# Two attentions beside a stream of matmuls: the maximum read as the exponential's bias, roundings on GpSimd, and a changed order of exponentials and fetches

## The chip, the cores and the metric

The kernel runs on one core of a Trainium2 chip. The metric is device time in microseconds of one execution; the figure of a kernel is the median of several runs. The engines are TensorE (PE, its weight loads PEld), VectorE (DVE), ScalarE (ACT), GpSimd (POOL) and SyncE (SP), which here only issues DMAs. Other DMAs are issued from the queues of ScalarE and GpSimd.

## The reference

One layer of a streaming encoder on 512 tokens of 1024 channels, in float32. The change touches the two attentions at its start:

```python
(a_q, a_k, a_v, f_q, f_k, f_v, f_g, ...) = jnp.split(h @ w_in[l], cuts, axis=-1)
# differential attention: 4 heads, two score maps of 64 channels each, chunk-causal mask
s = einsum(q_blk, k) * 64 ** -0.5
p = softmax(where(mask, s, -inf))
a = p[:, :, 0] - lam * p[:, :, 1]
ya = rms_norm(a @ v)
# forgetting attention: 8 heads of 64 channels, causal, with a bias from the cumulated gates
log_f = log_sigmoid(f_g + b_fgt);  c = cumsum(log_f)
s = einsum(q_blk, k) * 64 ** -0.5 + c_q - c_k
p = softmax(where(causal, s, -inf));  yf = p @ v
```

Around them stand a convolution module, a gated short convolution, sigmoid gates and projections of the four branches, an output projection, a cross attention into 256 memory tokens and a gated MLP. All of that runs unchanged before, beside and behind the two attentions.

## The kernel before, in words

**Products.** Matrix products are taken as three fp32r matmuls, each float32 operand being split into a rounded high part and a low rest. `split` (lines 153 to 156) does it for a result in PSUM: ScalarE copies to the high part, VectorE subtracts. `split_weights` does it for weights (line 192 the ScalarE cast of 128x1024, line 193 the VectorE subtraction). High and low are rounded in writing them.

**The main stream.** `run_blocks` (line 209) runs a list of jobs in order. A job has a weights tile to be loaded and a body that issues its matmuls: a group of 24 matmuls of 512 columns for one block of output channels. Three jobs ahead, `fetch` loads the weights by SP and splits them; it stands in front of the body of the current job. Bodies evacuate their PSUM bank at the end. `main` (line 842) records the latest evacuation on ScalarE in `evacuations[0]`.

**The heads beside it.** `Background` holds generators, `a_task` (one for each head h of the first attention, lines 905 on) and `f_task` (one for each pair of heads p of the second, lines 1068 on). Between the matmuls of the main stream, `bg.tick` takes a step of them. Each has 4 steps with scores, one for each tile of 128 queries; query tile qt sees (qt + 1) * 128 keys, so the widths are 128, 256, 384 and 512. A step of `a_task` computes two score maps into PSUM; VectorE adds the mask, writes the sum to `e` and leaves its maximum in the small tile `st` (line 928). A VectorE operation of two columns multiplies the maxima by -1/8 (line 931); ScalarE takes the exponentials with that as bias and leaves their sums (line 933); a reciprocal and scalings follow (lines 935 to 938). `f_task` is the same with a bias tile that GpSimd makes from the cumulated gates (lines 1116 and 1118), the reduction in line 1122, the small operation in line 1125, the exponentials in line 1128.

**Turning the probabilities.** The values need the probabilities with keys on the partitions. The near heads (h = 3, p = 2 and 3) are turned by TensorE (`to_keys_major`). The far ones (h < 3, p < 2) are turned in squares of 32 by VectorE (line 848), stored to DRAM by SP (`put`, line 853) and fetched again in the turned order (`get`, line 860, into `ptl`). `split_in_place` then splits them: ScalarE casts `ptl` to `pth` (line 866, behind the latest evacuation) and VectorE subtracts (line 867). Two steps after its fetch, `values` multiplies them with v, half by half: the first half is for query tiles 0 and 1, the second for 2 and 3. The result is copied (line 947 in `a_task`), turned and normalised. GpSimd does the power operations of the norms (lines 277 and 280) and the clearing of parts of each head's `qk` tile (line 802).

**The values of the second attention** come from `vf_jobs`, four jobs with two channel tiles each (kb = 0 to 3). The last one evacuates eight PSUM banks (`done`, through `split`) and calls `forget_gates`, which computes the cumulated gates, writes them to DRAM (`crows`) and turns them.

**Order.** All this is program order. A scheduler at compile time, with a model of the engines, fixes from it the order of the instructions on each engine, program order being the priority. `tc.issue_after(x)` has what follows take its place behind instruction x in that order; it is no dependency in itself.

Of the kernel before, what the change touches and what calls it, by code (L numbers as in the profile page):

```python
# [17 lines left out]
F32 = mybir.dt.float32  # L18
F32R = mybir.dt.float32r
AF = mybir.ActivationFunctionType  # L20
# [5 lines left out]
P = 128  # L26
# [57 lines left out]
def hybrid_layer(ctx: ExitStack, tc: tile.TileContext, a: dict, out: bass.AP):  # L84
# [121 lines left out]
    def run_blocks(jobs, ahead=3):  # L206

        jobs = iter(jobs)  # L210
        pending = []

        def fetch():
            while True:
                job = next(jobs, None)
                if job is None:
                    return
                if job[1] is None:
                    pending.append((job[0]() if callable(job[0]) else job[0] or (), job[2]))
                else:  # L220
                    pending.append((load_weights(*job[:2], *job[3:]), job[2]))
                if job[0] is not None:
                    return

        for _ in range(ahead):
            fetch()
        while pending:
            if pending[0][0]:
                fetch()
            w, body = pending.pop(0)  # L230
            body(*w)
            bg.tick()

    def matmul(ps, lhs, rhs, start, stop):
# [624 lines left out]
    def get(d, n, pt, local):  # L859
        SP.dma_start(part_of(pt[1], n, local).bitcast(F32), d.rearrange("(a j) (b x) -> (j b) a x", j=32, b=4))  # L860

    def split_in_place(n, pt, local):
        hi, lo = (part_of(x, n, local) for x in pt)
        raw = lo.bitcast(F32)
        with tc.issue_after(evacuations[0]):
            A.copy(hi, raw)
        V.tensor_tensor(lo, raw, hi.bitcast(F32), ALU.subtract)

    def over_channels(ps, x):

# [24 lines left out]
    def a_task(h, qk, v):  # L895
        es, pt, av = {}, None, None
        far = h < 3
        yield 0.0, 3.0
        for step in range(8 if far else 6):
            if step in ((5, 7) if far else (3, 5)):  # L900
                if av is None:
                    av = bank("av")
                vh, vl = (x[:, :, h * P:(h + 1) * P] for x in v[0])
                with tc.issue_after(steps_of[0]) if far else ExitStack():
                    values(av, lambda kt: ((vh[:, kt], 0), (vh[:, kt], 1), (vl[:, kt], 0)), pt,
                           step // 2 - (2 if far else 1))
            cost = 0.0
            if far:
                for qt in SPLITS.get(step, ()):
                    split_in_place(qt + 1, pt, qt % 2)  # L910
                    cost += 0.1 + 0.15 * qt
                for qt in GETS.get(step, ()):
                    if qt % 2 == 0:
                        pt = pt_tiles()
                    get(es.pop(qt)[:, 0], qt + 1, pt, qt % 2)
            elif 1 <= step <= 4:
                if step in (1, 3):
                    pt = pt_tiles()
                to_keys_major(es.pop(step - 1)[:, 0], step, pt, (step - 1) % 2)
                cost += 0.1 + 0.15 * step  # L920
            if step < 4:
                qt, w = step, (step + 1) * P
                e = es[qt] = e4()
                st = m1p.tile([P, 8], F32, tag="st8", name="st8", bufs=4)
                for c in range(2):
                    ps = bank("sc")
                    scores(ps, qk, c, qt * P, w)
                    V.tensor_tensor_reduce(e[:, c, :w], ps[:, :w], mask_a[:, S - w:], scale=1.0,
                                           scalar=-3.0e38, op0=ALU.add, op1=ALU.max,
                                           accum_out=st[:, c:c + 1])  # L930
                V.tensor_scalar(st[:, 2:4], st[:, 0:2], -HD ** -0.5, None, ALU.mult)
                for c in range(2):
                    A.activation(e[:, c, :w], e[:, c, :w], AF.Exp, bias=st[:, 2 + c:3 + c],
                                 scale=HD ** -0.5, accum_out=st[:, 4 + c:5 + c])
                V.reciprocal(st[:, 6:8], st[:, 4:6])
                V.tensor_scalar(st[:, 7:8], st[:, 7:8], lam, None, ALU.mult)
                A.activation(e[:, 1, :w], e[:, 1, :w], AF.Copy, scale=st[:, 7:8])
                V.scalar_tensor_tensor(e[:, 0, :w], e[:, 0, :w], st[:, 6:7], e[:, 1, :w], ALU.mult,
                                       ALU.subtract)
                cost += 0.6 + 0.0035 * w  # L940
                if far:
                    turn_squares(e[:, 1, :w], e[:, 0, :w])
                    es[qt] = put(e[:, 1:], w)
                    cost += 0.0015 * w
            if step == (7 if far else 5):
                e = e4()
                A.copy(e[:, 0], av)
            yield cost, (6.0 if step == 5 else 4.0) if far else 3.5

        ps = bank("tr")  # L950
        for t in range(NT):
            transpose(ps[:, t * P:(t + 1) * P], e[:, 0, t * P:(t + 1) * P])
        A.activation(e[:, 1], ps, AF.Square, scale=1.0 / math.sqrt(P))
        ms = m1p.tile([P, NT], F32, tag="ms4", name="ms4", bufs=2)
        V.tensor_reduce(ms, e[:, 1].rearrange("p (t c) -> p t c", t=NT), AX.X, ALU.add)
        r = rstd_of(m1p, [ms], NT)
        V.tensor_tensor(e[:, 0].rearrange("p (t c) -> p t c", t=NT),
                        ps.rearrange("p (t c) -> p t c", t=NT),
                        r.unsqueeze(2).to_broadcast([P, NT, P]), ALU.mult)
        yield 1.5, 3.5  # L960
        ps2 = bank("tr")
        for t in range(NT):
            transpose(ps2[:, t * P:(t + 1) * P], e[:, 0, t * P:(t + 1) * P])
        if "a" not in y:
            y["a"] = (y8b(), y8b())
        split(ps2, y["a"][0][:, h], y["a"][1][:, h], half["dn"])
        yield 0.6, 0.0
# [5 lines left out]
    def vf_jobs(dst):  # L973
# [20 lines left out]
        for kb in range(4):  # L994
            def body(hi, lo, kb=kb):
                held.append((hi, lo))
                if kb == 0:
                    dst.append(m1p.tile([P, NT, 8, 2, HD], F32R, tag="v", name="v"))
                    dst.append(small["fz_raw"].rearrange("p (t h) -> p t h", t=NT))
                    ps.update({(t, g): bank(("mm", "av")[g]) for t in range(2) for g in range(2)})  # L1000
                products(kb, (0, 1))
                if kb < 3:
                    return
                done(0)
                done(1)
                bg.tick()
                ps.update({(t, g): bank(("mm", "av")[g]) for t in range(2, 4) for g in range(2)})
                for b in range(4):
                    products(b, (2, 3))
                    bg.tick()  # L1010
                done(2)
                done(3)
                forget_gates(dst[1])

            yield *cols(w_in, O_FV, BR + 8, kb * 2, 2), body

    def forget_gates(z_raw):
# [36 lines left out]
    def f_task(p, qk, v):  # L1054
# [19 lines left out]
        for step in range(8 if far else 6):  # L1074
# [33 lines left out]
            if step < 4:  # L1108
# [3 lines left out]
                for j in range(2):  # L1112
                    head = 2 * p + j
                    bias = m1p.tile([P, S], F32, tag="fbias", name="fbias", bufs=2)

                    G.tensor_scalar(bias[:, :w], ck[j][:, :w], -1.0, cq[:, qt, head:head + 1],  # L1116
                                    ALU.mult, ALU.add)
                    G.affine_select(out=bias[:, w - P:w], in_=bias[:, w - P:w], pattern=[[-1, P]],
                                    compare_op=ALU.is_ge, fill=BIG, base=0, channel_multiplier=1)
                    ps = bank("sc")  # L1120
                    scores(ps, qk, j, qt * P, w)
                    V.tensor_tensor_reduce(e[:, j, :w], ps[:, :w], bias[:, :w], scale=1.0,  # L1122
                                           scalar=-3.0e38, op0=ALU.add, op1=ALU.max,
                                           accum_out=st[:, j:j + 1])
                V.tensor_scalar(st[:, 2:4], st[:, 0:2], -HD ** -0.5, None, ALU.mult)
                turn_ready()
                for j in range(2):
                    A.activation(e[:, j, :w], e[:, j, :w], AF.Exp, bias=st[:, 2 + j:3 + j],
                                 scale=HD ** -0.5, accum_out=st[:, 4 + j:5 + j])
                V.reciprocal(st[:, 6:8], st[:, 4:6])  # L1130
                for j in range(2):
                    if j:
# [10 lines left out]

        e = e4()
        for j in range(2):
            A.copy(e[0:HD, j], av[j][HD:P])
            V.tensor_tensor(e[j * HD:(j + 1) * HD, 0], av[j][0:HD], e[0:HD, j], ALU.add)
        split(e[:, 0], y["f"][0][:, p], y["f"][1][:, p])
        yield 1.8, 0.0
# [741 lines left out]
```

## Time and profile before

| | before |
|---|---|
| median of 3 runs | 1050.71 us (1050.49 to 1051.55) |
| profiled execution | 1050.01 us |
| its span in the profile | 1048.2 us |
| granted TensorE clock, mean | 0.999 |
| instructions | 14451 |
| PE busy | 1037.6 us |
| DVE busy | 807.9 us |
| ACT busy | 508.5 us |
| POOL busy | 147.5 us |

The profile is of one execution. The ends of matmuls are modelled in it, so a busy TensorE may hold short waits; starts are recorded. Where the table and the views give a mean duration, it is of all instructions of a group. The first attention runs from about 225 to 350 us, the second from about 380 to 545 us, both beside products of the main stream.

### The profile page before, as it was taken

Reading aid. Unit: us, or ns where it says so; the run is one execution under the profiler, and the core shown is the slowest. Engines: PE = TensorE matmul, PEld = TensorE weight load, DVE = VectorE, ACT = ScalarE, POOL = GpSimd, SP = SyncE. Lnnn points to the kernel's source line nnn. Section 1 sums busy time; section 2 is a strip of 40 time slices with the busy share of each in tenths; the row PEclk is TensorE's granted clock in tenths of the full one; section 3 lists DMA queues with packets and bytes.
Section 4 is the critical chain, followed back from the end, with each engine's and each line's share of the span. In section 5 each row is a group of like instructions: output and inputs, shape, how many; then the busy total and the mean of one; then the engine's idle time right before and its main releaser. Section 6 shows DMA issues by size and latency. Waiting matters only on the chain.

```text
span 1048.2 us, 14451 instructions
## 1 busy us (share of the span) xinstructions
PE 1037.6 (99%) x5255; PEld 882.5 (84%) x5255; DVE 807.9 (77%) x1265; ACT 508.5 (49%) x838; POOL 147.5 (14%) x239
## 2 busy tenths in 40 slices
PE   8999999999999999999999999999999999999997
PEld 8888888888888988888888899998888888888886
DVE  7999998677768369876577898776767777667796
ACT  5322222376465356765443666655343333445662
POOL 4001000100000114432101031121112111111001
PEclk9999999999999999999999999999999999999999
DMA  8953333334433246642357734235577666726662
GB/s 272 315 158 90 102 100 101 99 85 122 137 103 110 61 122 186 181 136 81 101 160 265 237 124 137 63 104 189 191 241 225 217 224 218 220 81 183 215 215 81
DMA packets 182141, 163.86 MB, mean 156 GB/s; under 512 B 17151, under 2 KB 154092, under 8 KB 182069
## 3 DMA queue, kind: packets, MB, share of 16 engines
q1 hardware_dynamic: 173027, 131.18, 42.0%
q10 hardware_dynamic: 6482, 23.21, 6.2%
q0 software_dynamic: 2560, 8.54, 2.5%
q8 instruction: 41, 0.67, 0.3%
q14 instruction: 31, 0.25, 0.1%
HBM read 139.43 MB, written 23.48 MB: 155 GB/s over the span
## 4 chain that ended last, share of the span: by engine, by line
PE 98%; DVE 1%; DMA 0%; ACT 0%; issue 0%; POOL 0%; POOLq 0%; DVEq 0%; SPq 0%; ACTq 0%
PE ps_mm L235 53%; PE ps_av L235 30%; PE ps_sc L235 7%; PE ps_tr L235 4%; PE ps_tr L241 2%; PE ps_mm L453 1%; PE ps_av L453 1%; DMA xs<-in_x 0%; ACT e L735 0%; DVE qk L808 0%; PE ps_tr L437 0%; DVE o L1781 0%; PE ps_av L437 0%; ACT qk L806 0%; DVE e L848 0%
## 5 line engine op out<-in xcount | busy, mean ns | idle before, releaser
L192 ACT CAST wh<-wr 128x1024 fp32r<-128x1024 f32 (+1 forms) x140 | 146.6, 1048 | 261.5 <-PE ps_mm L235 158.2
L193 DVE TENSOR_TENSOR wl<-wr,wh 128x1024 fp32r<-128x1024 f32 (+1 forms) x140 | 174.7, 1249 | 85.5 <-ACT wh L192 85.3
L235 PE MATMUL ps_mm<-hth,wh 128*128 128x512 f32 (+1 forms) x616 | 230.5, 381 | 0.4 <-DVE qk L808 0.2
L235 PE MATMUL ps_mm<-hth,wl 128*128 128x512 f32 (+1 forms) x616 | 229.8, 379 | 0.0
L235 PE MATMUL ps_mm<-htl,wh 128*128 128x512 f32 (+1 forms) x616 | 229.7, 379 | 0.0
L235 PEld LDWEIGHTS ps_mm<-hth,wh 128*128 128x128 f32 x616 | 114.1, 188 | 21.9 <-ACT y L158 0.6
L235 PEld LDWEIGHTS ps_mm<-hth,wl 128*128 128x128 f32 x616 | 114.0, 188 | 21.4
L235 PEld LDWEIGHTS ps_mm<-htl,wh 128*128 128x128 f32 x616 | 114.0, 188 | 20.5
L235 PE MATMUL ps_av<-htl,wh 128*128 128x512 f32 (+1 forms) x328 | 122.5, 373 | 0.0
L235 PE MATMUL ps_av<-hth,wh 128*128 128x512 f32 (+1 forms) x328 | 122.4, 373 | 0.0
L235 PE MATMUL ps_av<-hth,wl 128*128 128x512 f32 (+1 forms) x328 | 122.3, 373 | 0.0
L688 DVE SCALAR_TENSOR_TENSOR y<-y,par,y 128x508 f32<-128x508 f32 (+29 forms) x120 | 82.9, 731 | 0.1
L235 PEld LDWEIGHTS ps_av<-hth,wl 128*128 128x128 f32 x328 | 61.7, 188 | 11.0
L235 PEld LDWEIGHTS ps_av<-htl,wh 128*128 128x128 f32 x328 | 61.6, 188 | 10.9
L235 PEld LDWEIGHTS ps_av<-hth,wh 128*128 128x128 f32 x328 | 61.6, 188 | 10.8
L1682 DVE TENSOR_TENSOR wl<-dw,wh 128x1024 fp32r<-128x1024 f32 x32 | 40.1, 1257 | 15.6 <-ACT wh L1681 15.4
L1681 ACT CAST wh<-dw 128x1024 fp32r<-128x1024 f32 x32 | 33.5, 1052 | 22.0 <-PE ps_mm L235 7.4
L1629 ACT ACTIVATE th<-c 128x512 f32<-128x512 f32 x22 | 13.9, 632 | 48.1 <-DVE c L615 48.1
L1116 POOL TENSOR_SCALAR fbias<-ck,cq 128x128 f32<-128x128 f32 (+3 forms) x32 | 27.0, 847 | 70.4 <-DVE st L1122 63.2
L615 DVE SCALAR_TENSOR_TENSOR c<-ps_mm,par,c 128x510 f32<-128x510 f32 (+1 forms) x44 | 32.8, 745 | 0.7
L235 PE MATMUL ps_mm<-y8b,wh 128*128 128x512 f32 x96 | 30.7, 396 | 0.0
L235 PE MATMUL ps_mm<-y,wh 128*128 128x512 f32 x96 | 30.6, 393 | 0.0
(484 smaller groups left out, 2092.4 us busy)
## 6 DMA issues: line engine op xcount, KB each, us to landing
wr<-in_w_up SPq DMA_DIRECT2D x44, 512.0 KB
wr<-in_w_in SPq DMA_DIRECT2D x38, 512.0 KB
wr<-in_w_gate SPq DMA_DIRECT2D x32, 512.0 KB
wp<-in_w_down ACTq DMA_DIRECT2D x22, 512.0 KB
sums<-wp ACTq DMA_DIRECT2D x22, 512.0 KB
dw<-sums SPq DMA_DIRECT2D x44, 256.0 KB
wr<-in_w_branch SPq DMA_DIRECT2D x16, 512.0 KB
wide<-in_w_out SPq DMA_DIRECT2D x12, 512.0 KB
```

The lines of the kernel that those rows point to most:

```text
L192: last_weights[:] = [order(A.copy(hi, raw[:, :n])).ins, low.tensor_tensor(lo, raw[:, :n], hi.bitcast(F32), ALU.subtract).ins]
L193: low.tensor_tensor(lo, raw[:, :n], hi.bitcast(F32), ALU.subtract).ins]
L235: steps_of[:] = [PE.matmul(ps, lhs, rhs, start=start, stop=stop).ins]
L241: turns.append(PE.transpose(ps, x, ident[:n, :n]).ins)
L453: keep(PE.matmul(banks[c][:, :S // 2], w[p == 1][:, k, c * P:(c + 1) * P], ht[p == 2][:, i * 4 + k, :S // 2], start=(i, p, k) == (0, 0, 0) ...
L615: ins = V.scalar_tensor_tensor(dst[:, s:], src[:, :S - s], w(k), dst[:, s:], ALU.mult, ALU.add)
L688: ins = V.scalar_tensor_tensor(dst[:, s:], src[:, :S - s], pc("conv_dw", k * 4 + j), dst[:, s:], ALU.mult, ALU.add)
L1116: G.tensor_scalar(bias[:, :w], ck[j][:, :w], -1.0, cq[:, qt, head:head + 1], ALU.mult, ALU.add)
L1629: A.activation(th, c[:, 0], AF.Silu)
L1681: A.copy(hi, x)
L1682: V.tensor_tensor(lo, x, hi.bitcast(F32), ALU.subtract)
```

## The change

It has four parts.

1. A body may have the mark `fetch_after`. `run_blocks` then fetches the next weights after that body and not before. Only the last job of `vf_jobs` (kb = 3) has it.
2. `split_in_place` takes an engine. The three far heads of `a_task` give it GpSimd, which then does the cast and the subtraction, without `issue_after`; the far pairs of `f_task` stay on ScalarE and VectorE.
3. The reductions of both attentions multiply by -1/8 and take the minimum: `e` holds the negated, scaled scores, and the accumulator holds the exponential's bias. The two-column operation is gone, and the exponentials have a scale of -1.
4. In `f_task`, `turn_ready` (the turning of the piece before) takes its place behind the last reduction; the exponentials and the final copy of the values take theirs behind the latest evacuation.

```diff
@@ run_blocks
         while pending:
-            if pending[0][0]:
+            w, body = pending.pop(0)
+            later = getattr(body, "fetch_after", False)
+            if w and not later:
                 fetch()
-            w, body = pending.pop(0)
             body(*w)
+            if later:
+                fetch()
             bg.tick()
@@ split_in_place
-    def split_in_place(n, pt, local):
+    def split_in_place(n, pt, local, engine=V):
         hi, lo = (part_of(x, n, local) for x in pt)
         raw = lo.bitcast(F32)
-        with tc.issue_after(evacuations[0]):
-            A.copy(hi, raw)
-        V.tensor_tensor(lo, raw, hi.bitcast(F32), ALU.subtract)
+        if engine is G:
+            G.tensor_copy(hi, raw)
+        else:
+            with tc.issue_after(evacuations[0]):
+                A.copy(hi, raw)
+        engine.tensor_tensor(lo, raw, hi.bitcast(F32), ALU.subtract)
@@ a_task
-                    split_in_place(qt + 1, pt, qt % 2)
+                    split_in_place(qt + 1, pt, qt % 2, G)
...
-                    V.tensor_tensor_reduce(e[:, c, :w], ps[:, :w], mask_a[:, S - w:], scale=1.0,
-                                           scalar=-3.0e38, op0=ALU.add, op1=ALU.max,
+                    V.tensor_tensor_reduce(e[:, c, :w], ps[:, :w], mask_a[:, S - w:], scale=-HD ** -0.5,
+                                           scalar=3.0e38, op0=ALU.add, op1=ALU.min,
                                            accum_out=st[:, c:c + 1])
-                V.tensor_scalar(st[:, 2:4], st[:, 0:2], -HD ** -0.5, None, ALU.mult)
                 for c in range(2):
-                    A.activation(e[:, c, :w], e[:, c, :w], AF.Exp, bias=st[:, 2 + c:3 + c],
-                                 scale=HD ** -0.5, accum_out=st[:, 4 + c:5 + c])
+                    A.activation(e[:, c, :w], e[:, c, :w], AF.Exp, bias=st[:, c:c + 1],
+                                 scale=-1.0, accum_out=st[:, 4 + c:5 + c])
@@ vf_jobs
+            body.fetch_after = kb == 3
             yield *cols(w_in, O_FV, BR + 8, kb * 2, 2), body
@@ f_task
-                    V.tensor_tensor_reduce(e[:, j, :w], ps[:, :w], bias[:, :w], scale=1.0,
-                                           scalar=-3.0e38, op0=ALU.add, op1=ALU.max,
-                                           accum_out=st[:, j:j + 1])
-                V.tensor_scalar(st[:, 2:4], st[:, 0:2], -HD ** -0.5, None, ALU.mult)
-                turn_ready()
+                    low = V.tensor_tensor_reduce(e[:, j, :w], ps[:, :w], bias[:, :w], scale=-HD ** -0.5,
+                                                 scalar=3.0e38, op0=ALU.add, op1=ALU.min,
+                                                 accum_out=st[:, j:j + 1])
+                with tc.issue_after(low.ins):
+                    turn_ready()
                 for j in range(2):
-                    A.activation(e[:, j, :w], e[:, j, :w], AF.Exp, bias=st[:, 2 + j:3 + j],
-                                 scale=HD ** -0.5, accum_out=st[:, 4 + j:5 + j])
+                    with tc.issue_after(evacuations[0]):
+                        A.activation(e[:, j, :w], e[:, j, :w], AF.Exp, bias=st[:, j:j + 1],
+                                     scale=-1.0, accum_out=st[:, 4 + j:5 + j])
...
-            A.copy(e[0:HD, j], av[j][HD:P])
+            with tc.issue_after(evacuations[0]):
+                A.copy(e[0:HD, j], av[j][HD:P])
```

## The prediction

> **What bounds the kernel now.** I read the page first: the busy times, the slices and the chain that ended last.
>
> ```profile
> span 1048.2 us, 14451 instructions
> PE 1037.6 (99%) x5255; PEld 882.5 (84%) x5255; DVE 807.9 (77%) x1265; ACT 508.5 (49%) x838; POOL 147.5 (14%) x239
> PEclk9999999999999999999999999999999999999999
> PE 98%; DVE 1%; DMA 0%; ACT 0%; issue 0%; POOL 0%; POOLq 0%; DVEq 0%; SPq 0%; ACTq 0%
> ```
>
> TensorE is busy for 1037.6 of 1048.2 us, the clock is full in every slice, and 98% of the chain that sets the end is matmuls. So the other engines' work is worth only what TensorE waits for it. The changed instructions lie between about 225 us (head 0 of the first attention) and 545 us (the last pair of heads of the second). The table of stretches for 200 to 545 us, its sum, is next, and then all that the list of TensorE's waits names in the whole run (engine, line, releaser; us in total, times, longest).
>
> ```profile
> sum 345.00, PE 344.43 PEld 292.73 DVE 245.55 ACT 197.54 POOL 60.33; mean PE 57.40 PEld 48.79 DVE 40.92 ACT 32.92 POOL 10.05
> PE ps_tr L437 <- DVE nt L432: 1.4, 1, 1.4
> PE ps_mm L394 <- DVE e L344: 1.3, 1, 1.3
> PE ps_mm L235 <- DVE qk L808: 0.2, 1, 0.2
> PE ps_tr L241 <- ACT e L947: 0.2, 1, 0.2
> ```
>
> In the changed 345 us, TensorE is idle for 345.00 − 344.43 = 0.57 us. Lines 394 and 437 are start and end of the kernel; only the two waits of 0.2 us lie here. A matmul's end is modelled, so a wait can also hide inside a busy row. For that I take the chain of waits, where 24 matmuls of 512 columns are one piece:
>
> ```profile
> 143.77 5.44 PE ps_mm L235 x24
> 220.68 5.71 PE ps_mm L235 x24
> 291.88 5.52 PE ps_mm L235 x24
> 441.69 5.74 PE ps_mm L235 x24
> ```
>
> Undisturbed they take 5.44 us. In the attention stage most take 5.46 to 5.56 us (small gaps at matmuls that carry a semaphore wait), and the two worst lose 5.71 − 5.44 = 0.27 and 5.74 − 5.44 = 0.30 us. The first lies ahead of the first changed instruction. That leaves little to be gained.
>
> **Part 1, the roundings of three heads go to GpSimd.** Each of the heads 0, 1 and 2 of the first attention has four pairs of cast (line 866, ScalarE) and subtraction (line 867, VectorE), one for each width. The groups of the two engines, by shape, between 200 and 560 us (busy us, mean ns):
>
> ```profile
> L866 ACT CAST pth<-ptl 128x512 fp32r<-128x512 f32 x7 | 4.1, 618 | 2.9 <-DMA ptl<-turned 2.9
> L866 ACT CAST pth<-ptl 128x384 fp32r<-128x384 f32 x7 | 3.4, 510 | 0.0
> L866 ACT CAST pth<-ptl 128x256 fp32r<-128x256 f32 x7 | 2.8, 407 | 3.3 <-DMA ptl<-turned 3.2
> L866 ACT CAST pth<-ptl 128x128 fp32r<-128x128 f32 x7 | 2.0, 295 | 3.4 <-DMA ptl<-turned 3.3
> L867 DVE TENSOR_TENSOR ptl<-ptl,pth 128x512 fp32r<-128x512 f32 x7 | 4.7, 686 | 1.9 <-ACT pth L866 1.9
> L867 DVE TENSOR_TENSOR ptl<-ptl,pth 128x384 fp32r<-128x384 f32 x7 | 3.7, 554 | 0.1
> L867 DVE TENSOR_TENSOR ptl<-ptl,pth 128x256 fp32r<-128x256 f32 x7 | 2.9, 431 | 0.8 <-ACT pth L866 0.8
> L867 DVE TENSOR_TENSOR ptl<-ptl,pth 128x128 fp32r<-128x128 f32 x7 | 2.0, 293 | 1.1 <-ACT pth L866 1.0
> ```
>
> Of each seven, three move. ScalarE loses 3 × (618 + 510 + 407 + 295) ns = 5.5 us and VectorE 3 × (686 + 554 + 431 + 293) ns = 5.9 us; neither is the bound. GpSimd gains 24 operations. It has run the subtraction with a rounded result before, at one width (line 426), but no rounding cast; I bound the cast by its nearest rows.
>
> ```profile
> L426 POOL TENSOR_TENSOR wa<-e,wa 128x512 fp32r<-128x512 f32 x4 | 5.1, 1306 | 1.4 <-ACT wa L423 1.4
> L590 POOL TENSOR_TENSOR qb<-qb,qa 128x256 f32<-128x256 f32 x11 | 12.6, 1144 | 0.9
> 424.96 0.69 POOL L1116 TENSOR_SCALAR fbias<-ck,cq 128x512 f32<-128x512 f32 x1 [4.00 <-DVE st L1122]
> 498.24 2.84 POOL L1116 TENSOR_SCALAR fbias<-ck,cq 128x512 f32<-128x512 f32 x2 [5.87 <-DVE st L1122]
> 499.39 1.21 DVE L193 TENSOR_TENSOR wl<-wr,wh 128x1024 fp32r<-128x1024 f32 x1
> 461.65 1.47 DVE L193 TENSOR_TENSOR wl<-wr,wh 128x1024 fp32r<-128x1024 f32 x1
> ```
>
> With its data to itself GpSimd takes one operand of 512 columns to a float32 result in 0.69 us, and subtracts 512 with a rounded result in 1.31 us. The cast lies between 0.69 us and, at the worst row for its width, line 590's 1144 ns for 256 columns; I take 0.69, the row with one operand. An estimate from these, in proportion: a 512 pair is 2.0 us, a 256 pair at least 0.35 + 0.65 = 1.0 us. Beside VectorE's subtraction of two SBUF operands (line 193) it is slower: two operations that should take 1.4 us take 2.84 us at 498.24 us, and line 193 in turn reaches 1.47 us at 461.65 where GpSimd's operation had begun first, against 1.21 us. So one collision costs either side up to about 1.2 us. The Trainium skill, "SBUF — State Buffer", section "Who interferes with whom", says that a VectorE instruction with two SBUF inputs contends with a GpSimd instruction that reads SBUF, and that whoever issues first makes the other wait in full. The rows agree on the direction; by the page each collision would cost the rest of the other's duration, which speaks against this change but alters no term below.
>
> Whether it costs time depends on TensorE's first use of each pair. In the built order the tightest place is head 1's first half. These rows of the timeline are before's (start, duration):
>
> ```profile
> 270.50 0.28 PE L235 MATMUL ps_av<-pth,v 128*128 128x256 f32 x1
> 273.36 0.28 PE L235 MATMUL ps_av<-pth,v 128*128 128x128 f32 x1
> 278.31 0.28 PE L235 MATMUL ps_av<-pth,v 128*128 128x256 f32 x1
> 270.22 0.64 DVE L848 STREAM_TRANSPOSE e<-e 128x256 f32<-128x256 f32 x1
> 270.93 0.33 SPq L853 DMA_DIRECT2D turned<-e  x1
> 274.84 0.41 ACT L866 CAST pth<-ptl 128x256 fp32r<-128x256 f32 x1 [0.77 <-DMA ptl<-turned]
> 269.49 1.10 POOL L802 MEMSET qk<- 64x512 f32 x2 [18.30 <-PE ps_sc L235]
> ```
>
> Before, head 0's second half runs from 270.50 to about 273.5 us and head 1's first half from 278.31. In after the second follows the first directly: by moving the blocks of matmuls, I place head 1's first cast use near 271.75 and its first use of the subtraction near 272.3 us. On the data's side, its widest piece is turned some 5 us earlier than at 270.22, for the exponentials' bias is there sooner and the turned head 0 no longer shares VectorE; so the turn ends near 265.5 us. From issue of the store (270.93) to the cast (274.84) passed 3.9 us, so the piece lands near 265.5 + 3.9 = 269.4 us. Line 193 is then in the way till about 269.8; the cast ends near 270.3 and the subtraction near 271.1 us. Slack: 1.4 and 1.2 us, no wait. The two memsets of 0.55 us (269.49, x2) stand ahead of these in GpSimd's queue but wait for scores that end before 266. Head 0's second half is rounded by about 265.2 against 270.5; head 2's by 335.3 against 338.6. Queued behind the roundings on GpSimd are only memsets and rstd operations that TensorE needs over 5 us later. Taken cost: 0.3 us, a quarter of the 1.2 us that one more collision would cost.
>
> **Part 2, the bias comes from the reduction.** 32 small operations vanish.
>
> ```profile
> L1125 DVE TENSOR_SCALAR st<-st 128x2 f32<-128x2 f32 x16 | 3.5, 222 | 0.2
> L931 DVE TENSOR_SCALAR st<-st 128x2 f32<-128x2 f32 x16 | 2.7, 168 | 0.1
> ```
>
> VectorE is relieved of 3.5 + 2.7 = 6.2 us, and each chain from scores to exponentials is about 0.2 us shorter. The reductions and exponentials keep their widths, so I give them their old durations. TensorE waits for none of the 32, so the worth is nothing by itself.
>
> **Part 3, one fetch later and exponentials behind the evacuation.** The fetch after the last values block brings in the same weights, only its DMA (SP), cast (ScalarE) and subtraction (VectorE) come after the evacuations; those weights are three jobs ahead, over 10 us. Behind the fetch on SP are only later weights. The evacuations and the forget gates' chain move up by about 3 us. The exponentials of the second attention get their place on ScalarE behind the latest evacuation; the lag of a whole step between a head's scores and their use covers it. The tightest such place, and the one place in this part where TensorE waits now:
>
> ```profile
> 502.68 0.62 ACT L1135 ACTIVATE e<-e,st 128x384 f32<-128x384 f32 x1 [0.23 <-DVE st L1130]
> 506.46 0.81 PE L241 MATMUL ps_tr<-ident,e 128*128 128x128 f32 x6
> 350.12 0.58 ACT L947 COPY e<-ps_av 128x512 f32<-128x512 f32 x1 [3.35 <-PE ps_av L235]
> 350.75 0.66 PE L241 MATMUL ps_tr<-ident,e 128*128 128x128 f32 x4 [0.21 <-ACT e L947]
> ```
>
> The probabilities are scaled by 502.68 + 0.62 = 503.3 us and turned by TensorE from 506.46: a slack of 3.1 us. In after, about 8 us of matmuls lie between the scores and the turn where 9.3 lay before, so 1.9 us are left.
>
> Two small stalls may go. One is the wait for the copy at line 947, 0.2 us at 350.75; counted from the four transposes before it (started at 349.92), it is 0.4 us. After, copy and transposes are about 3 us apart. The other is at 441.69 us, the 0.30 us above, which waits for VectorE's line 1176; about 0.3 us less stands ahead of it. Together −0.4 − 0.2 = −0.6 us.
>
> **The sum.** −0.6 + 0.3 = −0.3 us. The profiled execution took 1050.01 us (span 1048.2 and 1.8 around it), 0.7 us under the median of 1050.71. Against the median I forecast 1050.4 us, no change. A measurement of this kernel can tell about 0.2%, 2.1 us, from no change.
>
> **The rivals.**
>
> *GpSimd is late (slower).* If the rounding cast on GpSimd is much slower than line 1116's operation, or collisions with line 193 fall on both operations of a pair, head 1's first half is late, and everything on TensorE behind it. At line 590's 1144 ns for 256 columns and one line 193 ahead of each (1.2 us), the pair ends at 269.4 + 2 × 2.35 = 274.1 us against 272.3: a stall of 1.8 us. It decides from 1.2 us of lateness. With twice that price for the cast, the 512-wide pairs of heads 0 and 2 pass their slack of 3 to 5 us too, and the stall grows to 3 or 4 us. For it: no row shows the cast. Against: line 426 rounds its result at the price of a plain operation, and three heads need some 3 × 5.6 = 17 us of an engine that is 14% busy. I take 2.6 us: 1053.3 us.
>
> *The exponentials come too late (slower).* With an evacuation that itself waits for a group of 24 matmuls (5.44 us), an exponential behind it is up to 5.4 us late, and the slack of 1.9 us at the turn of 506.46 is overrun by 3.5 us: 1053.9 us. Against: in the built order only evacuations that are ready stand there.
>
> *The small gaps vanish (faster).* The attention stage's groups are 0.02 to 0.3 us longer than 5.44; if about half of the gaps and the two stalls went, some −2.4 us: 1048.0 us. Against: TensorE carries the same number of semaphore waits in both orders, 659 and 660.
>
> *The change does nothing of note:* the schedule shifts but not one wait is touched, 1050.7 us.
>
> **How the numbers follow.** The forecast has 0.52, the late GpSimd 0.22 (0.16 of it above 2.1 us), the late exponentials 0.13 (0.11 above), the vanished gaps 0.08 (0.06 beyond), nothing of note 0.05. Slower is 0.16 + 0.11 = 0.27, faster 0.06, within 0.2% 0.67. The range runs from 1049.0 us (1050.7 less the 0.6 us of the stalls, as much again from small gaps, and 0.5 us for the scatter of the runs) to 1053.8 us (the late GpSimd's 1053.3 and the same scatter), which leaves out most of the faster rival and about half of the late exponentials, some 0.15 with the late GpSimd's end.
>
> **What would show it.** Right: TensorE idle under 0.6 us between 200 and 545 us, no wait for GpSimd's tiles in its list, lines 931 and 1125 gone, GpSimd's casts near 0.35 to 0.7 us and subtractions near 0.65 to 1.3 us, no stall at 350.75. Wrong: a wait of values matmuls for GpSimd at head 1, or of transposes for ScalarE's exponentials.

## The result, and the profile after

The change makes the kernel slower: 1053.79 us (median of 9 runs, 1053.34 to 1055.61) against 1051.30 us for the kernel before (9 runs on the same chip). The ratio is 1.0025 with a 95% interval of 1.0016 to 1.0033, some 2.6 us. No change was forecast, at 1050.4 us.

The page after: span, busy times and the share of the chain by engine.

```profile
span 1052.5 us, 14408 instructions
PE 1038.7 (99%) x5255; PEld 882.4 (84%) x5255; DVE 801.3 (76%) x1221; ACT 505.4 (48%) x826; POOL 159.5 (15%) x263
PE 96%; DMA 2%; DVE 1%; issue 0%; ACT 0%; POOL 0%; POOLq 0%; DVEq 0%; SPq 0%; ACTq 0%
```

VectorE is busy 6.6 us less (12.1 were worked out from durations; its 44 operations fewer are right, but records of neighbouring operations overlap, so that a vanished one frees less than its duration, and some of the rest took longer), ScalarE 3.1 us less (5.5 were worked out), GpSimd 12 us more. TensorE does the same matmuls, and the chain now passes through DMAs for 2% of the span. The stretches from 200 to 548 us, their sum, and TensorE's waits in the whole run:

```profile
sum 348.00, PE 344.06 PEld 291.98 DVE 236.97 ACT 194.22 POOL 75.70; mean PE 57.34 PEld 48.66 DVE 39.50 ACT 32.37 POOL 12.62
PE ps_mm L238 <- DVE ge L1184: 3.0, 2, 2.0
PE ps_mm L397 <- DVE e L347: 1.3, 1, 1.3
PE ps_tr L440 <- DVE nt L435: 1.3, 1, 1.3
PE ps_mm L238 <- DVE qk L821: 0.7, 1, 0.7
PE ps_mm L238 <- DVE qk L811: 0.2, 1, 0.2
```

TensorE is idle for 3.94 us in the attention stage, where it was 0.57 us. The wait for line 947 is gone, as forecast, and three are new, none of them for GpSimd or for an exponential. All three are for VectorE's evacuation of a PSUM bank that the next group of matmuls needs: one for line 821 and two for line 1184, which are 818 and 1176 of before. (The wait for line 811, 808 of before, is an old one.) Counted from start to start of TensorE's instructions, against the usual distance, they are 0.83 us at 263, 1.25 us at 410.6 and 2.17 us at 445.8 us (0.29 us there before). The usual distance depends on the neighbours, so these counts are good to about 0.05 us. At 350.75 us the eight transposes take 0.79 us up to the next matmul, where they took 1.25 us, so 0.46 us went there. That is 3.5 us net, of the 4.3 us between the two profiled executions. Of the rest, 0.3 us lies in the first 30 us, which the change does not touch, and some 0.4 us in small gaps. The interval of the ratio, 1.7 to 3.5 us, just reaches the 3.5 us; the profiled execution of before was 1.3 us under its median.

**The wait at 445.8 us.** The rows of the kernel after, VectorE's and SyncE's, then the matmul that waits:

```profile
437.64 0.49 DVE L1140 TENSOR_SCALAR e<-e,st 128x512 f32<-128x512 f32 x1
440.54 2.07 DVE L851 STREAM_TRANSPOSE e<-e 128x512 f32<-128x512 f32 x2 [2.41 <-ACT e L1154]
442.54 1.17 DVE L193 TENSOR_TENSOR wl<-wr,wh 128x1024 fp32r<-128x1024 f32 x1
443.64 1.39 DVE L1155 TENSOR_TENSOR e<-ps_av,e 64x512 f32<-64x512 f32 x2
445.06 0.69 DVE L1184 SCALAR_TENSOR_TENSOR ge<-ge,ps_mm 128x512 f32<-128x512 f32 x1
437.59 0.36 SPq L856 DMA_DIRECT2D turned<-e  x1
445.81 0.50 PE L238 MATMUL ps_mm<-hth,wh 128*128 128x512 f32 x1 [2.01 <-DVE ge L1184]
```

The same place before:

```profile
436.54 0.68 DVE L1147 TENSOR_TENSOR e<-ps_av,e 64x512 f32<-64x512 f32 x1 [0.41 <-ACT e L1146]
434.77 0.36 SPq L853 DMA_DIRECT2D turned<-e  x1
437.64 2.09 DVE L848 STREAM_TRANSPOSE e<-e 128x512 f32<-128x512 f32 x2 [0.41 <-DMA turned<-e]
440.76 0.27 DVE L867 TENSOR_TENSOR ptl<-ptl,pth 128x128 fp32r<-128x128 f32 x1
440.96 0.67 DVE L1176 SCALAR_TENSOR_TENSOR ge<-ge,ps_mm 128x512 f32<-128x512 f32 x1
```

In both, the turns of the 512-wide piece wait until the store of the piece before has been read out of its buffer (the e tiles have three buffers). Before, the wait is 0.41 us, because VectorE fills it with the final additions of line 1147. After, the additions (line 1155) are placed behind the turns; VectorE stands idle for 2.41 us and has 1.39 us of additions between the turns and ge, where 0.27 us stood before. The bracket names the copy of line 1154, but the store issued at 437.59 ends at about the same time: 2.9 us later, as in the kernel before (434.77 to 437.64). It is the store: in ten traces (before, after and eight of the runs below) these turns start 2.9 to 3.3 us after that store is issued, and in one of them, a_nomin, they start at 441.71 us, when that copy, at 441.68 us, has only begun.

**The wait at 410.6 us.** After, then before:

```profile
401.17 0.37 SPq L176 DMA_DIRECT2D wr<-in_w_gate  x1
403.99 0.91 SPq L863 DMA_DIRECT2D ptl<-turned  x2
409.12 0.41 ACT L872 CAST pth<-ptl 128x256 fp32r<-128x256 f32 x1 [3.82 <-DMA ptl<-turned]
409.56 0.42 DVE L873 TENSOR_TENSOR ptl<-ptl,pth 128x256 fp32r<-128x256 f32 x1 [1.84 <-ACT pth L872]
409.90 0.68 DVE L1184 SCALAR_TENSOR_TENSOR ge<-ge,ps_mm 128x512 f32<-128x512 f32 x1
410.64 0.50 PE L238 MATMUL ps_mm<-hth,wh 128*128 128x512 f32 x1 [1.04 <-DVE ge L1184]
```

```profile
399.75 0.46 SPq L176 DMA_DIRECT2D wr<-in_w_gate  x1
404.82 0.91 SPq L860 DMA_DIRECT2D ptl<-turned  x2
405.98 0.69 DVE L1176 SCALAR_TENSOR_TENSOR ge<-ge,ps_mm 128x512 f32<-128x512 f32 x1
407.21 0.41 ACT L866 CAST pth<-ptl 128x256 fp32r<-128x256 f32 x1 [1.90 <-DMA ptl<-turned]
```

Before, ge stands ahead of the 256-wide subtraction. After, it stands behind the first of them, and VectorE idles 1.84 us for a piece that lands late: its fetch is issued at 403.99 us and used at 409.12 (5.1 us), against 404.82 and 407.21 (2.4 us) before. The transfer of 512 KB of weights was issued 2.8 us ahead of the fetch after, 5.1 us before. The packets in the traces can be told apart by their size: 1024 of 512 bytes for these weights, 1024 of 256 bytes for the fetch. Before, the last of the weights ended at 403.69 us and the first of the fetch started at 405.85. After, the weights ran from 402.79 to 408.34 us and the fetch from 405.46 to 409.26, so the two ran at the same time. No run changes this alone.

**The wait at 263 us.** After, then before:

```profile
261.08 0.56 DVE L934 CUSTOM_DVE_ANT_0 e<-ps_sc,mask_a 128x384 f32<-128x384 f32 x1 [0.94 <-PE ps_sc L238]
261.56 1.39 DVE L821 TENSOR_TENSOR qk<-ps_mm,qk 64x512 fp32r<-64x512 f32 x2
264.21 0.67 DVE L1184 SCALAR_TENSOR_TENSOR ge<-ge,ps_mm 128x512 f32<-128x512 f32 x1
263.09 0.71 PE L238 MATMUL ps_mm<-y,wh 128*128 128x512 f32 x2 [0.66 <-DVE qk L821]
```

```profile
260.46 0.68 DVE L1176 SCALAR_TENSOR_TENSOR ge<-ge,ps_mm 128x512 f32<-128x512 f32 x1
261.06 1.39 DVE L818 TENSOR_TENSOR qk<-ps_mm,qk 64x512 fp32r<-64x512 f32 x2
261.36 0.63 PE L235 MATMUL ps_mm<-y,wh 128*128 128x512 f32 x2
```

Line 818 itself is only 0.5 us later. But ge has moved behind it, and in the built program the second group of products (the matmul shown) takes another bank: before, the one that ge frees at about 261.1 us, after, the one that line 821 frees at 262.95. Which bank a tile gets is decided when the program is built. The traces do not name the bank; what they show is that before, this group started at 261.36 us, while line 818 was still at work, and that after, it started when line 821 had ended.

### The profile page after: what moved, and what is told of

Its sections match the earlier page's. It is cut to its first block, busy times and chain, and to the rows that moved or that the text cites. A ratio compares the mean times of both kernels' runs of the same rounds, so it can differ in the third digit from the quotient of the medians.

```text
span 1052.5 us, 14408 instructions
## 1 busy us (share of the span) xinstructions
PE 1038.7 (99%) x5255; PEld 882.4 (84%) x5255; DVE 801.3 (76%) x1221; ACT 505.4 (48%) x826; POOL 159.5 (15%) x263
## 4 chain that ended last, share of the span: by engine, by line
PE 96%; DMA 2%; DVE 1%; issue 0%; ACT 0%; POOL 0%; POOLq 0%; DVEq 0%; SPq 0%; ACTq 0%
PE ps_mm L238 51%; PE ps_av L238 30%; PE ps_sc L238 7%; PE ps_tr L238 4%; PE ps_tr L244 2%; DMA turned<-e 1%; PE ps_mm L456 1%; PE ps_av L456 1%; DMA ptl<-turned 0%; DMA xs<-in_x 0%; ACT e L738 0%; DVE qk L811 0%; DVE e L851 0%; DVE ge L1184 0%; DVE qk L821 0%
## 5 line engine op out<-in xcount | busy, mean ns | idle before, releaser
L1122 POOL TENSOR_SCALAR fbias<-ck,cq 128x128 f32<-128x128 f32 (+3 forms) x32 | 24.5, 772 | 74.5 <-DVE st L1128 68.3
```

## The experiments

The theory after the two traces, called D: the loss is TensorE waiting for VectorE's evacuations, which stand in VectorE's queue behind instructions that wait for DMAs or scores. The rivals: G, GpSimd is late or slows VectorE; E, the exponentials and the copy behind the evacuation. All comparisons are with the kernel before, run beside each. The table gives the ratio with its interval, and the waits in the one profiled execution of each kernel from start to start, in us. The stall at 350.75 us is not in it: it is there in b_copy, b_fpool and b_fpool_fmin, as before, and gone in the others.

| kernel | ratio (95%) | near 262 | 285 | 368 | 410 | 430 | 441 to 447 | 523 |
|---|---|---|---|---|---|---|---|---|
| before | 1 | | | | | | 0.29 | |
| after | 1.0025 (1.0016 to 1.0033) | 0.83 | | | 1.25 | | 2.17 | |
| a_nopool | 1.0025 (1.0015 to 1.0035) | | 0.68 | | 1.24 | | 2.14 | |
| a_nomin | 1.0058 (1.0043 to 1.0073) | 0.80 | | 2.09 | | | 0.43 + 2.41 | |
| a_nofetch | 1.0035 (1.0023 to 1.0046) | 0.84 | | | 0.66 | | 2.15 | |
| a_noorder | 1.0018 (1.0008 to 1.0027) | 0.83 | | | 1.16 | | 1.03 + 0.26 | |
| b_copy | 1.0015 (1.0005 to 1.0024) | | | | | 0.84 | 1.87 | |
| b_pool | 1.0035 (1.0024 to 1.0047) | 0.80 | | 1.88 | | 0.54 | 0.91 | |
| b_min | 1.0012 (1.0003 to 1.0021) | | 0.40 | | 0.83 | | 0.99 + 0.51 | |
| x_fpool | 1.0005 (0.9996 to 1.0015) | 0.83 | | | | | | 0.91 |
| x_fpool_nocopy | 1.0011 (1.0002 to 1.0020) | 0.83 | | | | | | 0.91 |
| b_fpool | 1.0006 (0.9997 to 1.0014) | | | | 0.36 + 0.78 (at 415) | 0.46 | | 1.09 |
| b_fpool_fmin | 1.0018 (1.0009 to 1.0027) | | | | 1.64 (at 398) | | | 0.87 |
| a_nocopy | 1.0014 (1.0005 to 1.0023) | 0.83 | | | 1.46 | | 0.37 + 1.40 | |

**One part out of the changed kernel.** First, GpSimd's part (a_nopool):

```diff
-                    split_in_place(qt + 1, pt, qt % 2, G)
+                    split_in_place(qt + 1, pt, qt % 2)
```

> The changed kernel with the roundings of heads 0 to 2 back on ScalarE and VectorE. The changed kernel's trace shows three new waits of TensorE for VectorE's evacuations: 0.8 us at 263 us (line 821), 1.25 us at 410.6 us (line 1184, behind a subtraction of a piece whose fetch landed late) and 2.2 us at 445.8 us (line 1184, behind turns that wait for a store, and behind the final addition; 0.3 us before). Theory D (VectorE's queue: the waits come from evacuations that stand behind instructions which wait for DMAs or scores): only the first of the three depends on GpSimd; it goes, the other two stay, about 1053 us. Rival G (GpSimd is late or slows VectorE): without it the time returns to before's, 1051 us. Rival E (the exponentials and the copy behind the evacuation): no change against the changed kernel, 1053.8 us with all three waits.

Measured: no gain at all. The wait at 263 us went, the other two stayed to within 0.03 us, and a new one of 0.68 us came at 285 us, again for ge. TensorE's waits, the row on ge:

```profile
PE ps_mm L238 <- DVE ge L1181: 3.5, 3, 2.0
```

GpSimd is not the cause of the waits at 410 and 445 us. Next, the old reduction and small operations in both attentions (a_nomin):

```diff
-                    V.tensor_tensor_reduce(..., scale=-HD ** -0.5, scalar=3.0e38, op0=ALU.add, op1=ALU.min, ...)
+                    V.tensor_tensor_reduce(..., scale=1.0, scalar=-3.0e38, op0=ALU.add, op1=ALU.max, ...)
+                V.tensor_scalar(st[:, 2:4], st[:, 0:2], -HD ** -0.5, None, ALU.mult)
```

> The changed kernel with the maximum and the two-column operations of lines 931 and 1125 back. Theory D: VectorE's order in the first attention is that of before, so the wait at 263 us goes; ge of 410.6 us stands behind two subtractions of fetched pieces and still waits 1 to 2 us; the wait at 445.8 us keeps its order and stays near 2 us. About 1053 us. Rival G: as the changed kernel, 1053.8 us, all three waits. Rival E: as the changed kernel.

Measured: 1.0058, far slower than any theory had it. Of theory D's three places, the wait at 410 us went (expected to stay), and the one at 263 us stayed (expected to go). A wait of 2.09 us for the evacuation of the values of the second attention came at 368.8 us. The wait at 447 us cost more than itself; the windows (TensorE's busy time and count, ..., then its granted clock, DMA share, GB/s) show why:

```profile
440.00:447.00 7.00, 4.54 (x22) 3.35 (x20) 5.22 (x7) 4.70 (x11) 0.00 (x0) 0.99 0.76 196
447.00:451.00 4.00, 4.00 (x11) 3.20 (x12) 4.00 (x13) 0.81 (x1) 2.70 (x4) 0.58 0.25 84
451.00:458.00 7.00, 7.00 (x36) 5.92 (x35) 3.07 (x5) 2.90 (x7) 0.00 (x0) 1.00 0.57 148
```

After this wait of 2.41 us (2.25 us without a matmul by the profile) the clock was 0.58 of full speed over 4 us, and matmuls of 512 columns started 0.43 us apart six times in a row where 0.23 us is usual. With the first of them that is another 1.6 us.

The mark on the last values job (a_nofetch):

```diff
-            body.fetch_after = kb == 3
```

> The changed kernel without the mark on the last values job, so that its fetch stands ahead of the body again. Theory D: the three places in VectorE's order are as in the changed kernel; the three waits stay, 1053.8 us. Rivals G and E: the same. A third idea, that the late fetch shifts the weights' transfers onto the turned pieces' fetches: then the wait at 410.6 us goes and the time falls by 1.2 us to 1052.6 us.

Measured: all three waits are there; the one at 410 us fell to 0.66 us. So the third idea holds for half of that wait, but the time did not fall: 1.0035, with an interval that overlaps the changed kernel's.

The order in the second attention (a_noorder):

```diff
-                with tc.issue_after(low.ins):
-                    turn_ready()
+                turn_ready()
...
-                    with tc.issue_after(evacuations[0]):
-                        A.activation(e[:, j, :w], ..., AF.Exp, ...)
+                    A.activation(e[:, j, :w], ..., AF.Exp, ...)
...
-            with tc.issue_after(evacuations[0]):
-                A.copy(e[0:HD, j], av[j][HD:P])
+            A.copy(e[0:HD, j], av[j][HD:P])
```

> The changed kernel without its third part in the second attention: turn_ready, exponentials and copy stand where they stood before. Theory D: the waits at 263 and 410.6 us stay (ge then even stands behind two subtractions of the late pieces, 1.2 to 2 us); at 445.8 us the final additions come ahead of the turns again and about 1.1 to 1.9 us of the 2.2 us go. About 1052.3 us. Rival G: 1053.8 us with all three. Rival E: 1051 us, the waits at 410.6 and 445.8 us both gone.

Measured: 1.0018 (expected 1052.3 us, or 1.001). The waits at 263 and 410 us stayed, the one at 445 us fell from 2.17 to 0.26 us as theory D has it. Rival E, which had 1051 us and the wait at 410 us gone, fell. But 1.03 us came back 3 us earlier, as a wait for ScalarE's ge:

```profile
PE ps_mm L238 <- DVE ge L1181: 0.9, 1, 0.9
PE ps_mm L238 <- ACT ge L1169: 0.8, 1, 0.8
```

**One part into the kernel before.** The copy alone (b_copy):

```diff
-            A.copy(e[0:HD, j], av[j][HD:P])
+            with tc.issue_after(evacuations[0]):
+                A.copy(e[0:HD, j], av[j][HD:P])
```

> The kernel before with one thing of the change: the final copy of the second attention's values takes its place behind the latest evacuation. Theory D (VectorE's queue): the final additions (line 1147, 1.39 us) then stand between the turns and ge of line 1176 in the place where the kernel before has one subtraction of 0.27 us; the wait at 441.7 us grows by 1.1 us from 0.3 to 1.4 us, all else stays: 1052.3 us beside 1051.3 of before. Rival: the addition is covered elsewhere (VectorE idle before the turns), no wait grows, and the time stays.

Measured: 1.0015, and the wait in its place grew to 1.87 us, more than the 1.4 us expected. A second one, not expected, came at 429 us. The rival fell: the addition is not covered.

```profile
PE ps_mm L235 <- DVE ge L1177: 1.7, 1, 1.7
PE ps_mm L235 <- DVE qk L818: 0.7, 1, 0.7
```

GpSimd's part alone (b_pool; `split_in_place` as after, called with G by `a_task`):

> The kernel before with only the roundings of heads 0 to 2 on GpSimd. Theory D: in VectorE's built order the evacuation in line 818 at about 262 us has lost the ge ahead of it and comes late for TensorE, a wait of 0.8 us as in the changed kernel; at 410 and 441 us little. The stall at 350.75 us goes (0.4 us). About 1051.7 us. Rival G (GpSimd is the cause): all of the loss, 1053.8 us. Third: nothing, 1051.3 us.

Measured: 1.0035 (1.0024 to 1.0047), at rival G's figure (1.0024) or above it, but not by G's mechanism. The wait at 262 us is there with 0.80 us as theory D said; 1.88 us more came at 368.7 us, which it had not seen. None of the waits is for a tile of GpSimd's:

```profile
PE ps_mm L235 <- DVE v L156: 1.7, 1, 1.7
PE ps_mm L235 <- DVE qk L818: 1.0, 2, 0.6
PE ps_mm L235 <- ACT ge L1167: 0.7, 1, 0.7
```

The wait at 368.7 us has its cause in ScalarE's queue. In this kernel the weights' cast in line 192 waits 3.67 us for its DMA, until 366.02 us, and all four casts of the values (line 155) stand behind it, the first at 366.97 us. Before, one of them stood ahead of that cast, at 364.50 us, and TensorE did not wait. In a_nomin all four stand behind, the first at 367.07 us; in the changed kernel (365.67 us) and in all the others one stands ahead, and none of them has this wait.

The minimum alone, in both attentions (b_min):

> The kernel before with only the minimum in place of the maximum and without the 32 two-column operations. Theory D: the shorter chain moves VectorE's order, and evacuations come to stand behind subtractions of late pieces: waits of 0.7 us near 285 us, 1.2 us near 410 us and 1.0 us near 441.8 us, as they stand in the changed kernel without GpSimd or without its third part; about 1053.5 us although VectorE does 6 us less. Rival: less work ahead of every exponential can only help, 1051 us.

Measured: 1.0012 (1.0003 to 1.0021), about 1.3 us slower, with 32 operations of together 6.2 us fewer on VectorE, whose busy time fell by 3.4 us. Waits came in the three places that were expected, at 285, 409 and 441 to 444 us, with 0.40, 0.83 and 0.99 + 0.51 us. The rival, that less work can only help, fell.

**The subtractions of fetched pieces out of VectorE's queue.** In the changed kernel, the far pairs of the second attention are rounded on GpSimd too, so VectorE's queue holds no subtraction that waits for a fetch (x_fpool):

```diff
-                        split_in_place(qt + 1, pts[j], qt % 2)
+                        split_in_place(qt + 1, pts[j], qt % 2, G)
```

> The changed kernel with the roundings of the second attention's far pairs on GpSimd as well, so that no subtraction of a fetched piece is left in VectorE's queue. Theory D: the wait at 410.6 us (behind such a subtraction) goes; at 445.8 us ge stands ahead of the turns and the additions in the built order, so that wait goes too; the wait of 0.8 us at 263 us stays. About 1051 us, if GpSimd keeps up. Rival G: with twice the roundings on GpSimd the loss grows, above 1055 us, with values matmuls that wait for GpSimd.

Measured: 1.0005 (0.9996 to 1.0015), level with before within what these runs can tell. The waits at 410 and 445 us are both gone, the one at 263 us is there to 0.01 us, and the far larger share of GpSimd makes no values matmul wait. A wait at 523 us, for line 1155, was not expected.

```profile
PE ps_av L238 <- DVE e L1155: 0.7, 1, 0.7
PE ps_mm L238 <- DVE qk L821: 0.7, 1, 0.7
```

The same without the changed place of the copy (x_fpool_nocopy):

> The changed kernel, the second attention's far pairs rounded on GpSimd too, and the final copy of the values without its place behind the latest evacuation. With the far pairs on GpSimd alone, two waits of TensorE were left: 0.8 us at 263 us and 0.9 us near 523 us, the latter for the final addition behind that copy. Theory D: the second goes, the first stays (the second group of products still takes the bank that line 821 frees); 0.9 us less than the kernel with the copy behind, level with before or up to 0.5 us above it. Rival: the copy is not the cause at 523 us, and the wait stays.

Measured: 1.0011 (1.0002 to 1.0020), and the wait at 523 us is unchanged, 0.91 us; the rival was right, the copy is not its cause. It appears in every kernel here with the far pairs on GpSimd.

Only the far pairs on GpSimd, in the kernel before (b_fpool):

> The kernel before with one thing alone: the roundings of the second attention's far pairs on GpSimd, those of heads 0 to 2 where they were. Theory D: in the built order of VectorE every ge stands ahead of what waits for DMAs, and at 262 us the order is that of before; no new wait, and the 0.3 us at 441.7 us go: level with before, 0.3 us less at best. Rival G (roundings on GpSimd cost TensorE time): 1 to 3 us above before, with values matmuls that wait for GpSimd.

Measured: 1.0006 (0.9997 to 1.0014). Level within the interval, but not for the reason given: the 0.29 us at 441.7 us went and others came, among them the only two waits for GpSimd in this study:

```profile
414.42 0.39 PE L235 MATMUL ps_av<-ptl,v 128*128 128x256 f32 x1 [0.19 <-POOL ptl L870]
415.71 0.39 PE L235 MATMUL ps_av<-ptl,v 128*128 128x256 f32 x1 [0.56 <-POOL ptl L870]
```

Its trace has 2.4 us of waits more than that of before, but the ratio allows 1.5 us at most. So the waits of one profiled execution are not always those of the median; here the runs went from 1051.04 to 1054.26 us.

The same with the minimum in the second attention (b_fpool_fmin):

> The kernel before with the far pairs of the second attention rounded on GpSimd and the minimum in that attention alone. Theory D: no ge stands behind a piece that waits for a DMA in VectorE's built order, so the minimum's shorter chain does no harm here: level with before, within 0.5 us, where the minimum in both attentions with VectorE's roundings lost about 1.3 us. Rival: the minimum is bad by itself, 1 us or more above before.

Measured: 1.0018, against the expectation. No ge waits behind a fetched piece, but a wait of 1.64 us for line 818 came at 398 us. Taking one kind of blocker out of VectorE's queue does not make the minimum harmless.

Last, the changed kernel with only the copy put back (a_nocopy):

> The changed kernel with only the final copy put back to its old place. The copy alone, in the kernel before, made the wait at 444 us 1.9 us long. Theory D: here the additions leave the place ahead of ge, but in the built order two subtractions and the split of the result (0.28 + 0.68 + 0.42 = 1.38 us) take it, and the turns still wait for the store of the piece before; so the wait stays near 2.1 us and the time at the changed kernel's 1053.8 us. Rival E (the copy is the cause of that wait): it goes, 1.9 us less, 1052 us.

Measured: 1.0014 (1.0005 to 1.0023), with an interval that overlaps the changed kernel's, and the wait at 445 us at 1.40 us with 0.37 us ahead of it, in place of 2.17. Neither theory had that: in this trace the copy is 0.4 us of the wait net, the lateness of the turns and what else stands ahead of ge is the rest. The profiled execution was this kernel's slowest, 1055.32 us against a median of 1053.83, so the 0.4 us is no firm figure.

No kernel of these is faster than the kernel before.

**Which part brings which wait.** Read by columns, the table answers this. The wait near 262 us is in all eight kernels that have heads 0 to 2 on GpSimd, and in none of the six without, before included. The one near 410 us is in the six that have the minimum in both attentions and the far pairs of the second attention on ScalarE and VectorE, and in no other. A wait of 1.87 us or more near 445 us is in the five that have the copy behind the evacuation and the far pairs on VectorE; 1.40 us of it are left in a_nocopy. The one at 368 us is in the two with GpSimd's part and the maximum, the one at 523 us in the four with the far pairs on GpSimd.

## Why the prediction was wrong

**The bound was right.** TensorE is at 99% in both, and the worth of everything else is what TensorE waits for it. So was the size of what could be won: the stall at 350.75 us went, for 0.46 us where 0.4 was taken.

**That 1053.79 us lies inside the range is luck.** The range ended at 1053.8 us because of a late GpSimd, with 1053.3 us, and the scatter of the runs. The changed kernel's trace shows no late GpSimd; the loss has another cause. Both slower rivals (GpSimd late, exponentials late) named waits that did not come.

**Part 1, GpSimd, was right on GpSimd.** The cast, of which no row was known, takes 0.64 us for 512 columns where 0.69 was taken, the subtraction 1.31. The tightest place came out as worked out:

```profile
270.06 0.47 POOL L869 CAST pth<-ptl 128x256 fp32r<-128x256 f32 x1 [2.19 <-DMA ptl<-turned]
270.61 0.74 POOL L873 TENSOR_TENSOR ptl<-ptl,pth 128x256 fp32r<-128x256 f32 x1
271.86 0.28 PE L238 MATMUL ps_av<-pth,v 128*128 128x256 f32 x1
273.87 0.28 PE L238 MATMUL ps_av<-ptl,v 128*128 128x256 f32 x1
```

The cast ends at 270.53 us (forecast 270.3), the subtraction at 271.35 (271.1). Head 0's second half begins at 271.86, and the first use of the subtraction for head 1 is at 273.87 us, late enough by 2.5 us. The forecast had 272.3 us for that use and a slack of 1.2 us; 0.8 us of the difference is the new wait at 263 us. The 0.3 us set aside there were not spent. The rival of a late GpSimd fell with it. The price of a collision, up to about 1.2 us for either side, was misread: its rows give 1.4 us for GpSimd's two operations together (2.84 against 1.4) and 0.26 us for VectorE's (1.47 against 1.21). Between 200 and 560 us line 193's 51 subtractions of 1024 columns took 1237 ns on average, against 1238 before; its four of 1040 columns took 1412 against 1238.

**The failed step is the place of VectorE's evacuations.** For each part the prediction followed the probabilities: when they are ready and when TensorE uses them. It gave VectorE's relief of 12 us no term and the 32 vanished operations a worth of nothing "by itself", and the stall at 441.69 us a gain of 0.2 us because "about 0.3 us less stands ahead of it". But what TensorE came to wait for is the evacuations in lines 818 and 1176 (821 and 1184 after), and these stand in one queue with turns and subtractions that wait for DMAs, and with the final additions. In each of the kernels here, an operation that vanished or moved changed the order of that queue elsewhere too. In the changed kernel 2.07 us of turns with a wait of 2.41 us ahead and 1.39 us of additions precede that ge. The term was −0.2 us; the place measured +1.9 us. The terms for the evacuations at 263 and 410.6 us, +0.8 and +1.25 us, are missing from the sum.

**The minimum was mis-sized at 0.** Alone it costs about 1.3 us (0.3 to 2.2), through the order that it sets off. Its rows are as forecast: reductions and exponentials have their old durations, and the two-column operations are gone.

**Part 3 missed the copy.** The exponentials behind the evacuation made no wait in the changed kernel, and that rival fell. The copy behind the evacuation, for which the prediction had no term, made a wait of 1.87 us when it alone was put into the kernel before. The other things of part 3 (the late fetch, the turns behind the last reduction, the exponentials' place) were not tried alone in the kernel before.

**The parts do not add.** Alone, GpSimd's part costs 1.0035, the copy 1.0015 and the minimum 1.0012; together they would come to some 6.5 us, and the whole change costs 2.6 us. Each builds another order with other waits.

What stays open: how far the waits of one profiled execution stand for all runs of a kernel (b_fpool and a_nocopy show that they need not), and why the weights' transfer near 402 us was slower after than before.

## What to carry to other kernels

Where one engine is at 99%, look first at who frees its banks, and read that engine's queue as a whole: an evacuation behind an operation that waits for a DMA turns the DMA's lateness into a stall. A relief of an engine that is not the bound was worth nothing here and cost time, since it changed the order in which everything else was placed. The effects of the parts did not add up; the built order of each kernel has to be read for each bank that is handed back.

## What the runs showed of the hardware

- GpSimd's rounding cast is about as fast as ScalarE's: 644 ns for 128x512 against 618 ns. Its subtraction is 1.9 times VectorE's (1311 against 686 ns).

```profile
L873 POOL TENSOR_TENSOR ptl<-ptl,pth 128x512 fp32r<-128x512 f32 x3 | 3.9, 1311 | 0.2
L869 POOL CAST pth<-ptl 128x512 fp32r<-128x512 f32 x3 | 1.9, 644 | 4.1 <-DMA ptl<-turned 4.1
```

- In a_nomin, a wait of 2.41 us brought the clock down to about half for some 3.4 us (0.58 of full speed over 4 us); in the changed kernel's profiled execution, one of 2.17 us did not. The Trainium skill, "TensorE: Matmul & The Clock Gate", Part 1, has the clock fall after an idle window of about 3.4 us; here less was enough, and the measurement decides. With the 1.6 us of slower matmuls, that wait of 2.41 us cost about 4.0 us.
